# Between pooling and cross-attention: the last token block's norm and transposes, and the first key weights, take other places

## The chip, the cores and the metric

The kernel runs on one core of one Trainium2 chip. The metric is the device time of one execution in microseconds (us); lower is better. Engines are named as the profile names them: PE (matmul and transposes), DVE (vector), ACT (scalar), POOL (GpSimd) and SP, whose queue issues most of the loads.

## The reference, cut to what matters

Two decoder layers run over 512 tokens of 1024 features. Each layer is: half-step feed-forward and norm, token mixer and norm, cross-attention into 256 memory tokens and norm, half-step feed-forward and norm. The mixer of layer 0 is differential attention; that of layer 1 is the pooling mixer. The change lies in layer 1, from the end of its first feed-forward to the first queries of its cross-attention:

```python
def pool_mixer(x, w_grp, b_grp, scale):          # windows 2, 4, 8, 16
    pooled = stack(moving_mean(x, w) for w in windows) - x
    y = einsum('bsgc,gcd->bsgd', pooled, w_grp) + b_grp
    return y.reshape(B, S, D) * scale

x = layer_norm(a * x + pool_mixer(x, ...), ...)

def memory_cross_attention(x, mem, wq, wkv, wo):  # 4 heads of 256
    q = x @ wq;  k, v = split(mem @ wkv, 2)
    p = softmax(q @ k.T * 256 ** -0.5)
    return (p @ v) @ wo
```

## The kernel before, in words

Tokens lie in four blocks of 128 rows, `X[0]` to `X[3]` (in the trace and in the instruction order `X` or `X_74` to `X_77`). All products are made in three passes of float32 that is rounded to the PE's format: an operand is split into a high part, which ACT casts (line 125), and a low part, which DVE gets by subtracting the high part from the source (line 126). So each weight tile costs one cast on ACT (`wh<-raw`) and one subtraction on DVE (`wl<-raw,wh`), and lines 210, 211 and 212 are high by high, high by low of the activations, and low of the weights by high.

A norm of one token block (`ln_token`) is a chain over three engines: DVE makes the mean (line 371), ACT the squares and the variance (lines 379 and 380), POOL the power -1/2 (`rstd`, line 381), and DVE two steps over 128x1024 elements (lines 383 and 385), in place in `X[t]`. Each normalised block then goes through PE transposes (`turn`, line 496, eight of 128x128 for one block) and is split again into `xh` and `xl`, which the query projection reads. `self.late` lists the blocks that have been normalised but not yet transposed; `turn_late(wait)` transposes all of them but the last `wait`.

The pooling mixer of layer 1 needs no transposes of its input. It splits `X[t]` into `xh` and `xl` directly, multiplies by band matrices (`pp`), and then POOL adds a bias to `X[t]` in place (`pool_weights`, line 1356). While its units run, keys and values of the memory for the first heads are made as the main stream (`early_kv`, with `xa_k` for keys and `xa_v` for values): K0, V0, K1, V1, then K2. K0 to V1 below are these weights and products. The mixer's units are woven between. Norms of the mixer are made block by block at the end of `pool_mixer`: for each block two sums, then the transposes of the block before, then the norm of this one. So block 3 is left in `late` when cross-attention begins.

There (`xa_main`) head 0's queries are projected in two column halves of the tokens, blocks 0 and 1 first, blocks 2 and 3 afterwards, each for two output tiles `c`. Between these two halves block 3 is transposed.

The order of instructions on each engine is fixed when the program is built. A scheduler lists them by priority and by its own estimates of when operands are ready. `tc.high_priority()` puts what is issued within it ahead of other ready work; `issue_after` (used by `behind` and `after`) holds an instruction back until another has been listed. In `xa_k` the casts and subtractions of the first head's key weights carry neither; `x_split`, the last split of the mixer's input, holds back those of a head whose `raw` weights were handed in when `then` is not given.

Of the kernel before, what the change touches and what calls it, by code (L numbers as in the profile page):

```python
# [109 lines left out]
class Trunk:  # L110
# [80 lines left out]
    def mm(self, name):  # L191
        return self.mmp.tile([P, S], F32, tag="mm", name=name)
# [1165 lines left out]
    def pool_mixer(self, layer, ln):  # L1358
        nc = self.nc
        bandh, bandf, bandl = self.bandh, self.bandf, self.bandl  # L1360

        self.new_xt()
        xs = [[], []]
        for t in range(NT):
            for half in range(2):
                j = 2 * (t % 2) + half
                x = self.xh[t // 2][:, j], self.xl[t // 2][:, j]
                self.x_split = self.split(x[0], x[1], self.X[t][:, half * S : (half + 1) * S])
                xs[half].append(x)
        pooled = []  # L1370
        mm = nc.tensor.matmul
        yield
        for c in range(KC):
            if c == 1:
                with self.tc.issue_after(split[1].ins):
                    self.pool_weights()
            g = c // 2
            half, o = c // 4, slice((c % 4) * P, (c % 4 + 1) * P)
            pp = self.aux("pp")
            with self.behind():  # L1380
                for t in range(NT):
                    xh, xl = (x[:, o] for x in xs[half][t])
                    n = BAND if t < NT - 1 else P
                    out = pp[:, t * P : t * P + n]
                    m = (bandf if t == 0 else bandh)[:, g, :n]

                    mm(out, xh, m, start=t == 0, stop=False, skip_group_check=True)
                    if t == 0:
                        m0 = bandl[:, g]
                        mm(out[:, :16], xh, m0, start=False, stop=False, skip_group_check=True)  # L1390
                    mm(out, xl, m, start=False, stop=t == NT - 1, skip_group_check=True)
            q = self.pair("pooled")
            split = self.split(q[0], q[1], pp)
            pooled.append(q)
            yield
        wg = self.wide(self.pool_w)
        self.begin_ln(layer, ln, 1.0)
        for t in range(NT):
            o = slice(t * P, (t + 1) * P)
            for half in range(2):  # L1400
                ps = self.aux("ps")
                for j in range(2):
                    g = half * 2 + j
                    for k in range(2):
                        q = pooled[2 * g + k]
                        self.mm3(
                            ps[:, j * 256 : (j + 1) * 256],
                            (q[0][:, o], q[1][:, o]),
                            wg[2 * g + k],
                            k == 0,  # L1410
                            k == 1,
                        )
                self.ln_add(t, half, ALPHA, ps)
                yield
            self.turn_late()
            self.ln_token(t)


    def load_memory(self, tag=None):
# [47 lines left out]
    def xa_k(self, w, h, raw=None, then=None, turn=True):  # L1467
        rk = raw or self.raw_cols(w, h * 256)
        ps = self.mm("pk").rearrange("p (c n) -> p c n", c=2)
        for j in range(2):  # L1470
            with self.after(self.x_split if raw and not then else ()):
                wk = self.cols(rk, j)
            if then and j == 1:
                then()
            for n, k in enumerate(self.mem_order):
                yield self.mm3(
                    ps[:, j], (wk[0][:, k], wk[1][:, k]), self.memT[k], n == 0, n == KC - 1
                )
        kt = self.kv_tiles((P, 2, MEM))
        if turn:  # L1480
            self.turn_late()
        with nullcontext() if turn else self.tc.high_priority():
            self.split(kt[0], kt[1], ps)
        return kt
# [79 lines left out]
    def xa_main(self, layer):  # L1564
        wq, wkv = self.a["xa_wq"][layer], self.a["xa_wkv"][layer]
        early = len(self.kv)
        for h in range(XA_H):
            if h >= len(self.kv):
                self.kv.append((yield from self.xa_kv(wkv, h)))
            kt, v = self.kv[h]  # L1570
            raw = self.raw_cols(wq, h * 256)
            qs = []
            ws = [self.cols(raw, c) for c in range(2)]
            ps = [self.mm("xq") for c in range(2)]
            for p in ((0, 2 * P), (2 * P, S)) if self.late else ((0, S),):
                for c in range(2):
                    yield from self.project(ps[c], ws[c], (p,))
                    self.turn_late(max(len(self.late) - 1, 0) if c == 0 else 0)
            for c in range(2):
                q = self.pair("q")  # L1580
                self.split_scaled(q[0], q[1], ps[c], (D // XA_H) ** -0.5)
                qs.append(q)
            self.heads.append((self.clock, (qs, kt, v)))
            if 0 < early and h + early < XA_H:
                self.kv.append((yield from self.xa_kv(wkv, h + early)))
        yield from self.to_tokens(self.oT, self.a["xa_wo"][layer], 0, 4, True, False, ALPHA)
# [174 lines left out]
```

## Time and profile before

| what | value |
|---|---|
| median of 3 runs | 1916.96 us (1916.87 to 1918.63) |
| the profiled execution | 1915.99 us |
| its span, first to last instruction | 1914.2 us |
| what lies around the span | 1.8 us |
| PE busy | 1898.0 us, 99% of the span |
| DVE busy | 1551.7 us, 81% |
| ACT busy | 1016.6 us, 53% |
| POOL busy | 319.3 us, 17% |
| mean granted PE clock | 0.999 |

The rows of the timeline give the start of an instruction in us from the span's start, its duration in us, the engine, the line, the output and inputs, and, where the engine sat idle before it, how long and for whom. Durations of neighbours overlap a little since engines pipeline; the pace of an engine is the distance from start to start.

### The profile page before, as it was taken

To read this page: it belongs to the slowest core of one execution; us is meant where nothing else is said; L and a number is where in the kernel's file an instruction comes from. 1 tells how busy PE (TensorE), PEld (TensorE's weight loads), DVE (VectorE), ACT (ScalarE), POOL (GpSimd) and SP (SyncE) were. 2 spreads that over 40 slices of the span, in tenths; PEclk is the share of its full clock that TensorE was granted. 3 is DMA by queue.
4 is the path that set the end of the run, shared out by engine and by line. 5 is a ranking of instruction groups with operands and counts; after the bars stand their busy time and mean duration, and the time that the engine had idled before them with its cause. 6 is when DMAs were issued, how large, how long until landed. Compare 5 with 4: busy or idle time off the path is not lost.

```text
span 1914.2 us, 32507 instructions
## 1 busy us (share of the span) xinstructions
PE 1898.0 (99%) x13088; PEld 1732.0 (90%) x13088; DVE 1551.7 (81%) x2250; ACT 1016.6 (53%) x1578; POOL 319.3 (17%) x282
## 2 busy tenths in 40 slices
PE   9999999999999999999999999999999999999998
PEld 8999998888879888999998999999898889999996
DVE  7888889888867558889888988898787568998886
ACT  6555454566745435655553655555455436555552
POOL 3112121111110002221220311212130012211210
PEclk9999999999999999999999999999999999999999
DMA  9978772332225317987785687878344438867861
GB/s 249 215 176 177 177 139 78 91 89 67 89 67 161 116 60 194 193 175 164 143 191 171 117 180 166 181 164 186 101 132 133 137 84 174 178 156 168 189 130 54
DMA packets 246743, 277.96 MB, mean 145 GB/s; under 512 B 8256, under 2 KB 212544, under 8 KB 246592
## 3 DMA queue, kind: packets, MB, share of 16 engines
q0 software_dynamic: 92928, 92.29, 31.5%
q1 hardware_dynamic: 153664, 183.59, 29.9%
q8 instruction: 103, 1.69, 0.4%
q14 instruction: 48, 0.39, 0.1%
HBM read 273.75 MB, written 2.10 MB: 144 GB/s over the span
## 4 chain that ended last, share of the span: by engine, by line
PE 82%; DVE 11%; ACT 3%; DMA 2%; issue 1%; POOL 1%; SPq 0%; DVEq 0%; ACTq 0%; POOLq 0%
PE x L210 7%; PE x L211 7%; PE x L212 7%; PE z L210 4%; PE z L211 4%; PE z L212 4%; PE ps L210 4%; PE ps L212 4%; PE ps L211 4%; PE px L212 2%; PE px L210 2%; PE px L211 2%; PE y L212 2%; PE y L210 2%; PE y L211 2%; PE pz L212 1%
## 5 line engine op out<-in xcount | busy, mean ns | idle before, releaser
L715 POOL DMA_DIRECT2D ra<-in_ffn_w_in_dram x132 | 170.8, 1316 | 981.8 <-DVE wl L722 966.2
L720 ACT CAST wh<-ra 128x1024 fp32r<-128x1024 f32 x176 | 185.1, 1054 | 206.9 <-PE x L211 65.7
L722 DVE TENSOR_TENSOR wl<-ra,wh 128x1024 fp32r<-128x1024 f32 x176 | 214.2, 1222 | 66.5 <-ACT wh L720 66.1
L210 PE MATMUL x<-xe,wh 128*128 128x256 f32 x704 | 194.8, 277 | 0.0
L211 PE MATMUL x<-xe,wh 128*128 128x256 f32 x704 | 194.6, 276 | 0.0
L212 PE MATMUL x<-xe,wl 128*128 128x256 f32 x704 | 194.5, 276 | 0.0
L720 ACT CAST wh<-rc 128x1024 fp32r<-128x1024 f32 x132 | 138.9, 1053 | 101.6 <-PE x L211 41.4
L125 ACT CAST wh<-b 128x1024 fp32r<-128x1024 f32 x112 | 117.8, 1051 | 130.5 <-PE x L211 67.2
L722 DVE TENSOR_TENSOR wl<-rc,wh 128x1024 fp32r<-128x1024 f32 x132 | 160.0, 1220 | 24.9 <-ACT wh L720 24.9
L126 DVE TENSOR_TENSOR wl<-b,wh 128x1024 fp32r<-128x1024 f32 x112 | 136.8, 1221 | 40.2 <-ACT wh L125 40.2
L210 PE MATMUL x<-xh,wh 128*128 128x256 f32 x536 | 148.5, 277 | 0.0
L211 PE MATMUL x<-xl,wh 128*128 128x256 f32 x536 | 148.2, 276 | 0.0
L212 PE MATMUL x<-xh,wl 128*128 128x256 f32 x536 | 148.2, 276 | 0.0
L211 PEld LDWEIGHTS x<-xe,wh 128*128 128x128 f32 x704 | 132.3, 188 | 1.4
L210 PEld LDWEIGHTS x<-xe,wh 128*128 128x128 f32 x704 | 132.1, 188 | 1.3
L212 PEld LDWEIGHTS x<-xe,wl 128*128 128x128 f32 x704 | 132.2, 188 | 0.0
L126 DVE TENSOR_TENSOR wl<-raw,wh 128x1024 fp32r<-128x1024 f32 x64 | 82.2, 1288 | 42.0 <-ACT wh L125 41.2
L211 PEld LDWEIGHTS x<-xl,wh 128*128 128x128 f32 x536 | 100.7, 188 | 0.7
L210 PEld LDWEIGHTS x<-xh,wh 128*128 128x128 f32 x536 | 100.6, 188 | 0.7
L212 PEld LDWEIGHTS x<-xh,wl 128*128 128x128 f32 x536 | 100.6, 188 | 0.0
L125 ACT CAST wh<-raw 128x1024 fp32r<-128x1024 f32 x64 | 66.4, 1048 | 60.6 <-PE xq L211 20.2
L210 PE MATMUL z<-xe,wh 128*128 128x256 f32 x352 | 97.4, 277 | 0.0
(451 smaller groups left out, 6289.7 us busy)
## 6 DMA issues: line engine op xcount, KB each, us to landing
ra<-in_ffn_w_in_dram POOLq DMA_DIRECT2D x132, 512.0 KB, 6.9
rc<-in_ffn_w_in_dram SPq DMA_DIRECT2D x88, 512.0 KB, 5.9
b<-in_ffn_w_out_dram SPq DMA_DIRECT2D x76, 512.0 KB, 4.8
ra<-in_ffn_w_in_dram SPq DMA_DIRECT2D x44, 512.0 KB, 5.0
rc<-in_ffn_w_in_dram POOLq DMA_DIRECT2D x44, 512.0 KB, 7.5
raw<-in_xa_wkv_dram SPq DMA_DIRECT2D x16, 1024.0 KB, 5.4
raw<-in_da_w_qkv_dram SPq DMA_DIRECT2D x16, 512.0 KB, 5.2
raw<-in_xa_wq_dram SPq DMA_DIRECT2D x8, 1024.0 KB, 5.2
```

The lines of the kernel that those rows point to most:

```text
L125: self.nc.scalar.copy(hi, src),
L126: self.nc.vector.tensor_sub(lo, src, hi.bitcast(F32)),
L210: self.first_mm = mm(out, w[0], x[0], start=start, stop=False, skip_group_check=again)
L211: mm(out, w[0], x[1], start=False, stop=False, skip_group_check=again)
L212: self.last_mm = mm(out, w[1], x[0], start=False, stop=stop, skip_group_check=again)
L715: nc.gpsimd.dma_start(t, source(*block), accum_op=ALU.add)
L720: hi = nc.scalar.copy(v[0], raw)
L722: lo = nc.vector.tensor_sub(v[1], raw, v[0].bitcast(F32))
```

## The change

Three edits. In `pool_mixer` the norm of the last token block (`t > 2`) is issued with high priority. In `xa_k` the casts and subtractions of the first early head's key weights (K0, the call with `then`) are issued with high priority. In `xa_main` the remaining late blocks are transposed after the fourth of the eight contraction steps of the second output tile (`c` = 1), and no longer after the eighth.

```diff
@@ pool_mixer
             self.turn_late()
-            self.ln_token(t)
+            with self.tc.high_priority() if t > 2 else nullcontext():
+                self.ln_token(t)
@@ xa_k
         for j in range(2):
-            with self.after(self.x_split if raw and not then else ()):
+            with self.tc.high_priority() if then else self.after(self.x_split if raw else ()):
                 wk = self.cols(rk, j)
@@ xa_main
             for p in ((0, 2 * P), (2 * P, S)) if self.late else ((0, S),):
                 for c in range(2):
-                    yield from self.project(ps[c], ws[c], (p,))
-                    self.turn_late(max(len(self.late) - 1, 0) if c == 0 else 0)
+                    for k, ns in enumerate(self.project(ps[c], ws[c], (p,))):
+                        yield ns
+                        if c and k == 3:
+                            self.turn_late()
+                    if c == 0:
+                        self.turn_late(max(len(self.late) - 1, 0))
```

On DVE, at the end of layer 1's first feed-forward: `wl<-raw,wh` are the lows of K0's two weight tiles (the first two) and V0's two (the last two), `xl<-X_76,xh` the lows of block 2, and `X_77,sums` with `mean` the last sum and the mean of block 3.

```order
-L126 TENSOR_TENSOR wl<-raw,wh 128x1024
-L126 TENSOR_TENSOR xl<-X_76,xh 128x512 x2
-L126 TENSOR_TENSOR wl<-raw,wh 128x1024
+L126 TENSOR_TENSOR wl<-raw,wh 128x1024 x2
+L126 TENSOR_TENSOR xl<-X_76,xh 128x512
 L362 SCALAR_TENSOR_TENSOR X_77,sums<-X_77,ps 128x512
-L126 TENSOR_TENSOR wl<-raw,wh 128x1024
-L371 TENSOR_SCALAR mean<-sums 128x1
-L126 TENSOR_TENSOR wl<-raw,wh 128x1024
+L126 TENSOR_TENSOR xl<-X_76,xh 128x512
+L371 TENSOR_SCALAR mean<-sums 128x1
+L126 TENSOR_TENSOR wl<-raw,wh 128x1024 x2
```

K0's second tile moved ahead of both halves of block 2's lows, the sum came between these halves, and the mean went ahead of both of V0's tiles. ACT casts K0's second tile right behind the first, ahead of block 2's highs.

On DVE, at the start of cross-attention: `xl<-pt` are the lows of transposed blocks 2 and then 3, `X_77` with `mean,gb` and `rstd,gb` the two steps of block 3's norm, `kv<-pk` the lows of K2, and `wl<-raw` first V2's two weight tiles and then one of head 1's query weights.

```order
-L126 TENSOR_TENSOR xl<-pt,xh 128x4x128
+L383 SCALAR_TENSOR_TENSOR X_77<-X_77,mean,gb 128x1024
 L126 TENSOR_TENSOR kv<-pk,kv 128x512
-L126 TENSOR_TENSOR xl<-pt,xh 128x4x128
-L383 SCALAR_TENSOR_TENSOR X_77<-X_77,mean,gb 128x1024
-L126 TENSOR_TENSOR wl<-raw,wh 128x1024
 L385 SCALAR_TENSOR_TENSOR X_77<-X_77,rstd,gb 128x1024
-L126 TENSOR_TENSOR wl<-raw,wh 128x1024
-L126 TENSOR_TENSOR xl<-pt,xh 128x4x128 x2
-L126 TENSOR_TENSOR wl<-raw,wh 128x1024
+L126 TENSOR_TENSOR xl<-pt,xh 128x4x128 x4
+L126 TENSOR_TENSOR wl<-raw,wh 128x1024 x3
```

Ahead of block 3's second step stood two halves of block 2's lows, K2's lows and one weight tile; now only K2's lows stand between its two steps, and the lows of blocks 2 and 3 and V2's tiles follow.

On PE, the same place: `pt` are the transposes of block 3 (`X3_77`), `xq_16221` and `xq_16222` the query tiles `c` = 0 and `c` = 1. Before, they stand behind the last product of the first half of the tokens:

```order
L211 MATMUL xq_16222<-xl_15888,wh_16217 128x256
L212 MATMUL xq_16222<-xh_15886,wl_16218 128x256
L496 MATMUL pt_16247<-ident_78,X3_77 128x128 x4
L496 MATMUL pt_16254<-ident_78,X3_77 128x128 x4
L210 MATMUL xq_16221<-xh_15885,wh_16213 128x256
L210 MATMUL xq_16222<-xh_15885,wh_16217 128x256
L211 MATMUL xq_16221<-xl_15887,wh_16213 128x256
```

Now they stand behind the tenth of the 24 products of `xq_16222` in the first half:

```order
L212 MATMUL xq_16222<-xh_15885,wl_16218 128x256
L210 MATMUL xq_16222<-xh_15885,wh_16217 128x256
L496 MATMUL pt_16247<-ident_78,X3_77 128x128 x4
L496 MATMUL pt_16254<-ident_78,X3_77 128x128 x4
L211 MATMUL xq_16222<-xl_15887,wh_16217 128x256
L212 MATMUL xq_16222<-xh_15885,wl_16218 128x256
```

Fourteen products of `xq_16222` that PE did ahead of the transposes now follow them.

## The prediction

> **What bounds the kernel now.** I read the page first, then PE's timeline at the two places that the change touches, then DVE's, POOL's and ACT's rows beside them. The page says that PE is the bound:
>
> ```profile
> PE 1898.0 (99%) x13088; PEld 1732.0 (90%) x13088; DVE 1551.7 (81%) x2250; ACT 1016.6 (53%) x1578; POOL 319.3 (17%) x282
> ```
>
> So a change of order can only win back moments in which PE stands still, and these are small. At the first place, K0 and K1 on PE:
>
> ```profile
> 1393.96 0.28 PE L211 MATMUL pk<-mem0l,wh 128*128 128x256 f32 x1
> 1394.69 0.39 PE L212 MATMUL pk<-mem0h,wl 128*128 128x256 f32 x1 [0.45 <-DVE wl L126]
> ...
> 1397.39 0.28 PE L210 MATMUL pk<-mem0h,wh 128*128 128x256 f32 x1
> 1397.51 0.28 PE L211 MATMUL pk<-mem0l,wh 128*128 128x256 f32 x1
> 1398.13 0.39 PE L212 MATMUL pk<-mem0h,wl 128*128 128x256 f32 x1 [0.34 <-DVE wl L126]
> ...
> 1408.66 0.28 PE L211 MATMUL pk<-mem0l,wh 128*128 128x256 f32 x1
> 1409.11 0.39 PE L212 MATMUL pk<-mem0h,wl 128*128 128x256 f32 x1 [0.17 <-DVE wl L126]
> ```
>
> The pace is 0.12 us from start to start (1397.39 to 1397.51). PE reaches the low part of a weight tile before DVE has made it three times: for K0's first tile (0.73 instead of 0.12, so 0.61 us lost), for its second (0.62: 0.50 lost) and for K1's first (0.45: 0.33 lost). Together 1.44 us.
>
> At the second place PE ends the first half of head 0's queries and wants block 3's transposes:
>
> ```profile
> 1444.56 0.28 PE L212 MATMUL pk<-mem6h,wl 128*128 128x256 f32 x1
> ...
> 1446.02 0.28 PE L212 MATMUL pk<-mem6h,wl 128*128 128x256 f32 x1
> ...
> 1449.88 0.28 PE L210 MATMUL xq<-xh,wh 128*128 128x256 f32 x1
> ...
> 1451.47 0.28 PE L212 MATMUL xq<-xh,wl 128*128 128x256 f32 x1
> 1452.49 1.09 PE L496 MATMUL pt<-ident,X 128*128 128x128 f32 x8 [0.74 <-DVE X L385]
> ...
> 1454.77 0.28 PE L212 MATMUL xq<-xh,wl 128*128 128x256 f32 x1
> ```
>
> From 1444.56 to 1446.02 PE did eight transposes (block 2's) and two products: 1.46 us with next to no waiting. From 1451.47 to 1454.77 it did eight transposes and three products: 3.30 us. The third product costs 0.11 ((1451.47 - 1449.88) / 14 products), so this stretch would take 1.57 us without waits, and 1.73 us are lost: first to DVE's last step on block 3, then to its highs and lows after the transposes.
>
> **Second place: early norm, transposes amid the first half.** DVE and ACT before:
>
> ```profile
> 1445.90 1.22 DVE L126 TENSOR_TENSOR wl<-raw,wh 128x1024 fp32r<-128x1024 f32 x1
> 1447.04 0.68 DVE L126 TENSOR_TENSOR xl<-pt,xh 128x512 fp32r<-128x512 f32 x1
> ...
> 1448.83 1.27 DVE L383 SCALAR_TENSOR_TENSOR X<-X,mean,gb 128x1024 f32<-128x1024 f32 x1
> 1450.03 1.22 DVE L126 TENSOR_TENSOR wl<-raw,wh 128x1024 fp32r<-128x1024 f32 x1
> 1451.16 1.28 DVE L385 SCALAR_TENSOR_TENSOR X<-X,rstd,gb 128x1024 f32<-128x1024 f32 x1
> ```
>
> ```profile
> 1446.00 0.19 ACT L379 ACTIVATION_READ_ACCUMULATOR sq<-X,mean 128x1 f32 x1
> ...
> 1447.52 0.22 ACT L380 ACTIVATE var<-var 128x1 f32<-128x1 f32 x1
> 1447.62 2.00 ACT L125 CAST wh<-raw 128x1024 fp32r<-128x1024 f32 x2
> 1453.18 0.59 ACT L125 CAST xh<-pt 128x512 fp32r<-128x512 f32 x1 [3.56 <-PE pt L496]
> ```
>
> By the new order the first step on block 3 takes the place of the split at 1447.04; the squares that it has to wait for ended at 1446.19. It paces at 1.20 (1448.83 to 1450.03), K2's lows at 0.60 ((1448.83 - 1447.04) / 3), so the second step starts at 1448.84 and ends 1.28 later, at 1450.12, and no longer at 1452.44. POOL's power stands between: the variance comes one cast earlier, about 1447.1, and the power can be ready when the second step's turn comes (price below).
>
> PE gets to its new place after the product at 1449.88, that is at 1449.99. Against 1450.12 it waits 0.13 at most. The transposes' own work is unchanged. Of the 1.73 us I take 1.7 as won.
>
> What is late next there? The 14 products that now follow the transposes (1.59 us) cover the highs and lows. The highs begin 0.69 after the transposes (1452.49 to 1453.18 before), so at 1450.8; block 2's lows run from 1450.04 to 1451.2, block 3's from about 1451.4 to 1452.7. PE starts the second half at about 1452.8 and first reads only the first half of the features. Some 0.6 us of cover; if it went, PE would wait for just the excess. V2's lows, before at 1450.03 and after, move to about 1452.8 to 1455.0, far ahead of their product:
>
> ```profile
> 1460.40 0.36 PE L210 MATMUL pv<-wh,mem0h 128*128 128x256 f32 x1
> ```
>
> V2's buffer is thus freed some 1.5 us later, and on SP's queue the next load, K3, goes out that much later than here, while ACT casts it 11 us on:
>
> ```profile
> 1453.60 0.37 SPq L238 DMA_DIRECT2D raw<-in_xa_wkv_dram  x1
> ```
>
> ```profile
> 1464.81 1.05 ACT L125 CAST wh<-raw 128x1024 fp32r<-128x1024 f32 x1 [3.31 <-issue]
> ```
>
> With 1.7 us off that cast and 1.5 us on the load, 8 of these 11 us are left for a transfer of 5 to 7: nothing.
>
> **First place: K0 with priority.** DVE and POOL before:
>
> ```profile
> 1393.41 1.22 DVE L126 TENSOR_TENSOR wl<-raw,wh 128x1024 fp32r<-128x1024 f32 x1
> ...
> 1395.75 2.33 DVE L126 TENSOR_TENSOR wl<-raw,wh 128x1024 fp32r<-128x1024 f32 x1
> ...
> 1398.61 1.70 DVE L126 TENSOR_TENSOR wl<-raw,wh 128x1024 fp32r<-128x1024 f32 x1
> ...
> 1401.81 1.28 DVE L383 SCALAR_TENSOR_TENSOR X<-X,mean,hr 128x1024 f32<-128x1024 f32 x1 [0.24 <-ACT sp L379]
> 1403.54 1.29 DVE L385 SCALAR_TENSOR_TENSOR X<-X,rstd,sr 128x1024 f32<-128x1024 f32 x1 [0.44 <-POOL rstd L381]
> ...
> 1406.98 4.30 DVE L126 TENSOR_TENSOR wl<-raw,wh 128x1024 fp32r<-128x1024 f32 x2 [0.17 <-ACT wh L125]
> ```
>
> ```profile
> 1395.38 3.85 POOL L1356 TENSOR_TENSOR X<-X,p 128x512 f32<-128x512 f32 x2 [3.81 <-DVE xl L126]
> 1402.09 1.41 POOL L381 TENSOR_TENSOR rstd<-var,mhalf 128x1 f32<-128x1 f32 x1 [2.86 <-ACT var L380]
> ...
> 1447.88 0.55 POOL L381 TENSOR_TENSOR rstd<-var,mhalf 128x1 f32<-128x1 f32 x1 [4.55 <-ACT var L380]
> ```
>
> K0's first tile is already DVE's next work at 1393.41, behind block 3's first sum, and stays there: its 0.61 us remain. The second follows at once, about 1394.6, and is ready at 1395.8, 1.8 us before PE asks. So the stall of 0.50 goes.
>
> But this is not yet won. DVE's chain here runs on to block 3's first norm, to K1's casts behind it on ACT, and to the low part for which PE waits at 1409.11. Whatever PE gains at 1398 it loses there unless this chain ends earlier too. Its work is the same, so only its delays count. Before: a subtraction that takes 1.22 takes 2.33 and 1.70 while POOL adds the bias to block 2 (1.11 and 0.48 lost), then 0.24 and 0.44 of waiting for ACT and POOL: 2.27 us. After: POOL's first half-add can start only behind the first half of block 2's lows, so it falls on the second half of these lows, and the second half-add on one of V0's two tiles. Each collision cost about 0.9 to 1.1 (4.30 for two that need 2.44: 0.93 each; or 1.11): 1.9 to 2.2 us. The two waits go, since the mean now precedes V0's tiles. So the chain gains 0.1 to 0.4. Against it: the power took 1.41 beside DVE's step and 0.55 alone; if it now lies beside V0's second tile as well, 0.3 to 0.5 us come back. I take +0.1, with bounds of -0.3 and, were all collisions gone, +1.1 (the stalls of 0.50 and 0.33, and 0.3 of the chain).
>
> The Trainium skill ("SBUF — State Buffer", section "Who interferes with whom") says that a DVE instruction with two SBUF inputs and a GpSimd instruction that reads SBUF exclude one another for a whole instruction. The trace agrees: 2.33 against 1.22. By that rule this place is worth about nothing; if the two shared the time evenly and the sums (which read PSUM) hid part of it, the chain would gain 0.8 and the total be 2.5.
>
> K0's buffer is freed about 2.4 us earlier, so SP sends K1's load and those behind it earlier; K1's cast waits for block 3 on ACT and gains nothing by it. ACT's cast of K0's second tile moves into time in which ACT sat idle ahead of block 2's highs. Later in this stage K1's or V1's casts change places with a pooled split by one position; PE shows no wait there: nothing.
>
> **Sum.** 1.7 + 0.1 = 1.8 us. The profiled execution took 1915.99, so 1914.2; the median of the runs lies 0.97 above it, 1916.96, and 1.8 less is 1915.2. A fifth of a percent, 3.83 us, is about what a measurement of this kernel can tell from no change: this forecast lies within it.
>
> **Rivals.**
>
> *Both places pay.* If POOL's adds fall into gaps, the first place gives 1.1 and the sum is 2.8: 1914.2. For it: DVE's sum on PSUM was not slowed beside POOL. Against: POOL's add is released by the very lows that DVE is working on.
>
> *The second place doesn't pay.* PE then waits amid the half as long as it did behind it: about 1916.9. It would need block 3 to be ready at 1451.7 or later, that is 1.6 us lost on DVE or POOL between 1447.0 and 1448.8. Only the power could do it: its 1.41 began beside a step on DVE; even so it is done about 0.6 after that step, when K2's lows end. I find no more than a few tenths.
>
> *Slower: the load of V2 holds ACT.* Block 3's highs stand behind V2's two casts on ACT. Before, they were wanted at 1453.18, now at 1450.8, so that V2's lateness, harmless so far, can hold PE. Its transfer and the spread of all these transfers:
>
> ```profile
> raw<-in_xa_wkv_dram SPq DMA_DIRECT2D x1, 1024.0 KB, 5.3
> ...
> DMA to landing us min/median/max: 5.1/5.4/11.8
> ```
>
> It lands about 0.5 before 1447.62, and two casts take 2.0. PE waits once the casts end after some 1452.2, a landing at 1450.2; the gain of 1.7 is eaten at 1451.9, a transfer of 10. At 11.8 it lands at 1453.6 and the kernel is 1.7 slower than before: 1918.7. Against it: nothing stands ahead of this load, whereas the one of 11.8 had three before it.
>
> **How the numbers follow.** Forecast 0.58, both places 0.15, second place fails 0.13, slower by V2's load 0.08, anything else 0.06. All stalls named come to 1.44 + 1.73 = 3.2 us, under 3.83, so faster by over 0.2% has only the unnamed and the spread of runs: 0.07. Slower by over 0.2% needs a still later load or the unnamed: 0.07. The rest, 0.86, is within 0.2%. The range goes from 1913.6 (3.2 us and a little spread) to 1918.0 (the second place fails and the runs lie as the slowest of before, 1918.63, nearly did).
>
> **What would show it.** Right: K0's second low part is on DVE directly behind the first; PE's wait near 1398 is gone, and a wait near 1409 (for K1's lows, or for block 3's lows in the first `pp` products) takes most of it back; two subtractions between 1396 and 1402 are still stretched to about twice their time; block 3's second step ends some 2.3 us earlier against PE; the transposes start with a wait of under 0.2, and the second half's first products with none. Wrong: transposes that wait for more than 0.5, the second half waiting for `xl` or `xh`, or PE at 1409 earlier than before by more than 0.5.

## The result, and the profile after

The changed kernel takes 1913.84 us (median of 19 runs, 1912.81 to 1915.63), the kernel before beside it 1917.37 (19 runs, 1915.35 to 1919.56); the ratio is 0.9983, with a 95% interval of 0.9976 to 0.9990. That is 3.5 us less by the medians and 1.9 to 4.6 by the interval; the forecast was 1.8. The profiled execution took 1912.81 us instead of 1915.99, its span 1911.0 instead of 1914.2.

The page of the changed kernel shows a PE as busy as before, with 1.6 us less in it:

```profile
span 1911.0 us, 32507 instructions
...
PE 1896.4 (99%) x13088; PEld 1731.1 (91%) x13088; DVE 1551.6 (81%) x2250; ACT 1017.8 (53%) x1578; POOL 319.9 (17%) x282
```

PE's timeline after, first place. The wait for K0's second low (1398.13 before) is gone, the one for its first and the one for K1's first are as they were, and there is a new one for V0's second tile:

```profile
1393.35 0.28 PE L211 MATMUL pk<-mem0l,wh 128*128 128x256 f32 x1
1394.10 0.38 PE L212 MATMUL pk<-mem0h,wl 128*128 128x256 f32 x1 [0.47 <-DVE wl L126]
...
1396.83 0.28 PE L211 MATMUL pk<-mem0l,wh 128*128 128x256 f32 x1
1396.94 0.28 PE L212 MATMUL pk<-mem0h,wl 128*128 128x256 f32 x1
...
1400.80 0.28 PE L210 MATMUL pv<-wh,mem4h 128*128 128x256 f32 x1
1401.32 0.39 PE L211 MATMUL pv<-wl,mem4h 128*128 128x256 f32 x1 [0.25 <-DVE wl L126]
...
1407.69 0.28 PE L211 MATMUL pk<-mem0l,wh 128*128 128x256 f32 x1
1408.14 0.39 PE L212 MATMUL pk<-mem0h,wl 128*128 128x256 f32 x1 [0.17 <-DVE wl L126]
```

From 1393.35 to 1408.14 are 14.80 us by the unrounded times; the same stretch of the program took 15.15 before (1393.96 to 1409.11). So 0.35 us were won here, of the 0.50 that the vanished stall had cost.

The second place on PE after. The transposes begin 0.11 behind the product ahead of them, without a wait, and nothing waits behind them either. One small wait is new, ahead of them: the first product of the second query tile (1448.01):

```profile
1443.60 0.28 PE L212 MATMUL pk<-mem6h,wl 128*128 128x256 f32 x1
...
1448.01 0.39 PE L210 MATMUL xq<-xh,wh 128*128 128x256 f32 x1
...
1449.16 0.28 PE L210 MATMUL xq<-xh,wh 128*128 128x256 f32 x1
1449.27 1.03 PE L496 MATMUL pt<-ident,X 128*128 128x128 f32 x8
1450.06 0.36 PE L211 MATMUL xq<-xl,wh 128*128 128x256 f32 x1
...
1452.15 0.28 PE L210 MATMUL xq<-xh,wh 128*128 128x256 f32 x1
```

The product of 1452.15 is as many matmuls from the start of the program as that of 1454.77 before. From 1443.60 it is 8.54 us by the unrounded times, before (from 1444.56) 10.21: 1.67 won. The new wait costs 0.23 within this stretch: the product of 1448.01 starts 0.23 behind the one ahead and 0.22 ahead of the next, at a pace of 0.11. It ends with DVE's lows of K2 (1447.27 + 0.69 = 1447.96), which now stand behind the first step of block 3's norm.

That makes 2.0 us. Between the two places, and from the second to the last product, the two profiles differ by less than 0.1 us. The third part stands where the change touches nothing: at the very end. The last product, before and after:

```profile
1905.91 0.28 PE L212 MATMUL ps<-ha,xe 128*128 128x256 f32 x1
```

```profile
1903.34 0.28 PE L212 MATMUL ps<-ha,xe 128*128 128x256 f32 x1
```

The span ends 8.3 us behind it before and 7.7 after, though the products and the additions there are the same. The DMA view of the last microseconds, first of before from 1908 to its end, then of after from 1905 to its end (GB/s in 40 slices; then a queue's packets and MB; then the issues and the median time from issue to landing):

```profile
GB/s 0 0 0 0 0 0 0 0 0 0 0 0 0 0 0 0 92 396 410 357 344 199 396 383 396 344 66 13 26 13 0 0 0 0 0 0 0 0 0 0
...
q14 instruction: 1, 0.01, 0.3%
...
out_dram<-X SPq DMA_DIRECT2D x2, 256.0 KB, 2.4
```

```profile
GB/s 0 0 0 0 0 0 0 0 0 0 0 0 0 0 0 0 0 0 0 0 300 423 382 314 410 396 396 355 396 123 0 0 0 0 0 0 0 0 0 0
...
out_dram<-X SPq DMA_DIRECT2D x2, 256.0 KB, 2.1
```

Before, one packet of instructions (queue 14, 8 KB) falls amid the write of the output, 5.6 us behind the start of the last product. After, that queue is silent here: its packet came 1.3 us ahead of the last product. So 0.35 + 1.67 + 0.6 = 2.6 us can be named in the traces. Another 0.6 of the profiled pair lies ahead of 1393.96, where both programs are alike. The profiled kernels below, all with that program, got to this product anywhere from 1391.58 to 1394.78 us, so this is put down to chance.

### The profile page after: what moved, and what is told of

Its sections match the earlier page's. It is cut to its first block, busy times and chain, and to the rows that moved or that the text cites. A ratio compares the mean times of both kernels' runs of the same rounds, so it can differ in the third digit from the quotient of the medians.

```text
span 1911.0 us, 32507 instructions
## 1 busy us (share of the span) xinstructions
PE 1896.4 (99%) x13088; PEld 1731.1 (91%) x13088; DVE 1551.6 (81%) x2250; ACT 1017.8 (53%) x1578; POOL 319.9 (17%) x282
## 4 chain that ended last, share of the span: by engine, by line
PE 83%; DVE 11%; ACT 3%; DMA 2%; issue 1%; POOL 1%; SPq 0%; DVEq 0%; ACTq 0%; POOLq 0%
PE x L210 7%; PE x L211 7%; PE x L212 7%; PE z L210 4%; PE z L211 4%; PE z L212 4%; PE ps L210 4%; PE ps L212 4%; PE ps L211 4%; PE px L210 2%; PE px L212 2%; PE px L211 2%; PE y L212 2%; PE xq L210 2%; PE xq L211 2%; PE xq L212 2%
```

## The experiments

Each stretch below is read from PE's timeline between products of the same number in the program, so what chance did ahead of 1394 doesn't enter. "First place" is 1393.96 to 1409.11 of before, "between" from there to 1444.56, "second place" from there to 1454.77, "end" from the start of the last product to the end of the span (all from unrounded times, so that a last digit can differ from the rows above). The last column compares the runs; the word behind a comma names the kernel that the edit was made to. From the end of the second place to the last product every kernel takes 451.0 to 451.4 us, in no order that follows the edits.

| kernel | first place | between | second place | end | ratio to before |
|---|---|---|---|---|---|
| before | 15.15 | 35.45 | 10.21 | 8.30 | |
| changed | 14.80 | 35.46 | 8.54 | 7.70 | 0.9983 [0.9976, 0.9990] |
| e1 norm alone | 15.14 | 35.45 | 8.49 | 7.72 | 0.9988 [0.9979, 0.9997] |
| e2 K0 alone | 14.80 | 35.45 | 10.22 | 8.31 | 0.9997 [0.9988, 1.0005] |
| e3 transposes alone | 15.14 | 35.46 | 10.22 | 8.30 | 1.0000 [0.9992, 1.0009] |
| e4 changed again | 14.81 | 35.45 | 8.54 | 7.70 | 0.9990 [0.9981, 0.9998] |
| e5 one wait, before | 15.16 | 35.49 | 10.18 | 8.32 | 0.9999 [0.9990, 1.0008] |
| e6 additions late, changed | 13.83 | 35.33 | 8.55 | 7.71 | 0.9979 [0.9970, 0.9988] |
| e7 first low, changed | 14.80 | 35.45 | 8.49 | 7.70 | 0.9982 [0.9974, 0.9991] |
| e8 both, changed | 13.21 | 35.79 | 8.54 | 7.70 | 0.9983 [0.9974, 0.9991] |
| e9 one instruction, before | 15.16 | 35.45 | 10.21 | 7.70 | 0.9994 [0.9985, 1.0004] |
| e10 additions late, before | 13.82 | 36.38 | 10.18 | 8.31 | 0.9996 [0.9986, 1.0006] |
| e11 changed, beside e12 | 14.80 | 35.45 | 8.49 | 7.71 | 0.9990 [0.9981, 0.9999] |
| e12 additions late, beside e11 | 14.18 | 35.32 | 8.49 | 7.72 | 0.9979 [0.9970, 0.9988] |

**The three edits, one by one (e1 to e3), and the whole (e4).** The first:

```diff
-            self.ln_token(t)
+            with self.tc.high_priority() if t > 2 else nullcontext():
+                self.ln_token(t)
```

> Only the norm of block 3 has priority; transposes and K0 are written as before. The order of instructions that this gives is the same on every engine as that of this edit with the edit on the transposes together. Theory A (the gain is the norm's, at the second place; the edit on the transposes moves nothing): PE gains 1.6 us between 1446 and 1461, as in the changed kernel, nothing at the first place; time 1.6 us under before. Theory B (the transposes' place matters): less than half of that, 0.8 us or under. Theory C (part of the measured 3.5 us comes from nowhere near the two places): start and tail differ from before by some tenths again, in either direction.

Measured: 1913.46 us beside 1915.76. The second place gives 1.72 and the end 0.58, the first nothing. So the end belongs to this edit.

The second:

```diff
-            with self.after(self.x_split if raw and not then else ()):
+            with self.tc.high_priority() if then else self.after(self.x_split if raw else ()):
```

> Only K0's casts and subtractions have priority. Theory A (DVE's collisions with POOL give back most at K1): PE's wait for K0's second tile goes (0.5 us), PE is 0.3 us ahead of before after K1's first tile, nothing more later; time 0.3 us under before, within noise. Theory B (the first place carries what the two profiles don't show): 1.5 us or more under before.

Measured: 1915.11 us, not to be told from before by the runs; by the stretches 0.34 at the first place and nothing anywhere else. PE's waits from 1380 to 1470 (us in all, how many, the longest) show the trade, two waits for K0 and K1 and a new one for V0, with block 3 waited for as ever:

```profile
PE pt L496 <- DVE X L385: 0.8, 1, 0.8
PE pk L212 <- DVE wl L126: 0.6, 2, 0.5
PE pv L211 <- DVE wl L126: 0.3, 1, 0.3
```

The third is the edit in `xa_main` alone:

```diff
-                    yield from self.project(ps[c], ws[c], (p,))
-                    self.turn_late(max(len(self.late) - 1, 0) if c == 0 else 0)
+                    for k, ns in enumerate(self.project(ps[c], ws[c], (p,))):
+                        yield ns
+                        if c and k == 3:
+                            self.turn_late()
...
```

> Only the transposes of block 3 are written after the fourth step of the second query tile. The scheduler gives the same order of instructions on every engine as before, so this is before once more: theory A: no change, within 0.5 us, and every wait of before; the profile's start (first 12 us) and tail differ from before's by up to 0.7 us all the same, which tells how much of the difference of two profiles is chance. Theory B (the edit on the transposes does something that the order doesn't show): a change of 0.5 us or more at 1450.

Measured: 1915.63 us, ratio 1.0000, all four stretches as before. The order of instructions of this kernel is that of before on every engine, and in the trace of e1, which lacks the third edit, PE's order is that of the changed kernel from first to last. So it is the norm's priority that moved the transposes on PE: the scheduler lists them when it believes block 3 to be ready, wherever the code asks for them.

The changed kernel once more, beside these:

> The changed kernel once more. Theory A (two places, 1.9 us; the rest of 3.5 is chance): the comparison on one chip gives 1.5 to 2.5 us under before, PE is again 0.3 and 1.6 us ahead at the two places, and start and tail differ from the first profile by some tenths. Theory B (the change moves start or tail too): 3 us or more under before again, with the same 0.7 us in the first 12 us and 0.6 in the tail.

Measured: 1913.10 us, ratio 0.9990, and the stretches of the first time. By the stretches the parts add up: 0.34 (e2) + 1.72 and 0.58 (e1) = 2.6; the whole gives 0.34 + 1.67 + 0.60 = 2.6.

**What shortens the end (e5, e9).** The trace of before has 607 instructions on SP, that of the changed kernel and of e1 has 608: the load of K3, sent at 1454.15, waits for one semaphore more, by an instruction of its own at 1447.28. e5 gave the kernel before one more wait on SP, on the load of head 0's query weights for a pooled cast (`cast_2`):

```diff
...
+            if layer == 1 and h == 0:
+                info = mybir.DependencyInfo(mybir.DependencyClass.Sync, mybir.DependencyReason.DATA)
+                self.tc.add_manual_dep(self.last_load.ins, self.cast_2.ins.name, info, reason="one_more_wait")
```

> Before, with one more wait on SP's queue: the load of head 0's query weights also waits for a cast on ACT that ended 1.5 us earlier, so nothing starts later and every engine's order is that of before. The changed kernel too has one instruction more on SP than before. Theory A (the 0.6 us by which the changed kernel's end after PE's last product is shorter comes from where a block of SP's instructions is fetched: in before this fetch falls amid the write of the output, with one instruction more it comes ahead of it): the end after the last product takes 7.1 us and not 7.7, the fetch of 8 KB on queue 14 lies ahead of the last product, all else as before, time 0.6 us under before. Theory B (the end is shorter because the norm's order changed): 7.7 us as before, no change in time.

Measured: 1915.53 us, the end 8.32. (The expectation's 7.7 and 7.1 count to an event of SP some 0.6 ahead of the end of the span; they are the 8.3 and 7.7 of the table.) This does not decide, since the trace still has 607 instructions on SP: that load had two waits, and a third one went into an instruction that was there already. In the changed kernel it was a load with three waits that got a fourth. e9 did just that, on another load (the twentieth from line 238, sent at 1401.60 in before), for the last cast of weights ahead of it, with the order on all engines as before:

```diff
...
+        if self.loads == 20:
+            info = mybir.DependencyInfo(mybir.DependencyClass.Sync, mybir.DependencyReason.DATA)
+            self.tc.add_manual_dep(self.last_load.ins, self.last_cast.ins.name, info, reason="one_more_wait")
...
```

> The kernel before, with one more wait on the load that already waits for three things (the second head's first load of keys and values after the early ones, at 1401.6 in the trace of before); a fourth wait costs SyncE an instruction of its own, so that SyncE runs 608 instead of 607. The order on every engine is that of before. Theory A (the 0.58 us at the end hang on how many instructions SyncE has run: with one more, its next 8 KB of instructions are fetched before the last products instead of amid the write of the output): from the start of the last product to the end of the last instruction 7.7 us as in the changed kernel instead of 8.3, the fetch some 1.3 us ahead of that product instead of 5.6 us after it, and nothing else, so about 0.6 us under before. Theory B (the end is shorter because block 3's part of the program got shorter or because PE reached the end earlier): 8.3 us and no change.

Measured: 608 instructions on SP, the end 7.70, the other stretches as before to 0.02 us. The runs give 1914.36 beside 1916.01, ratio 0.9994 [0.9985, 1.0004]; 0.6 us is 0.9997, so they neither confirm nor exclude it, and the trace decides. Its last product, the DMA view of the stretch just ahead of it (1901.5 to 1903.4) and of the end:

```profile
1903.42 0.28 PE L212 MATMUL ps<-ha,xe 128*128 128x256 f32 x1
```

```profile
q14 instruction: 1, 0.01, 1.3%
```

```profile
out_dram<-X SPq DMA_DIRECT2D x2, 256.0 KB, 2.1
```

The packet lies ahead of the last product and the write lands in 2.1 us, as in the changed kernel. The other traces fit: the five with 607 instructions on SP have the packet 5.6 us behind the last product and an end of 8.30 to 8.32, the nine with 608 have it 1.2 to 1.4 ahead and an end of 7.70 to 7.72. So 0.6 us of the change's gain came from one instruction more on SP, whatever this instruction does. How the packet slows the end isn't settled. The last output packet ends 0.50 us earlier without it, which is most of the 0.6. SP sends the second half of the write 0.08 later with it (4.59 behind the last product in before, 4.51 after), and this half takes 2.56 us to land instead of 2.04, so most of the loss lies in the transfer; what in it is held up was not tried.

**What holds the first place (e6, e7, e8, e10).** e6 holds POOL's additions to blocks 2 and 3 back until the first pooled split:

```diff
...
-                nc.gpsimd.tensor_tensor(x, x, bs, ALU.add)
+                add = nc.gpsimd.tensor_tensor(x, x, bs, ALU.add)
+                if t > 1:
...
+                    self.tc.add_manual_dep(add.ins, behind.ins.name, info, reason="bias_late")
...
```

> The changed kernel, with POOL's bias adds on blocks 2 and 3 held back until K1's low parts and the first pooled split are done on DVE (nothing is left out). Theory A (these adds exclude DVE's subtractions with two operands in SBUF and so gave back most of the first place's gain): the three stretched subtractions, 1.47, 3.46 for two and 4.30 for two, take 0.7, 2.4 and 2.4; PE's waits for V0's second tile (0.4) and K1's first (0.33) go; PE is 0.8 us further ahead at 1410 than in the changed kernel; time 0.8 us under it unless the adds then stretch V1's tiles. Theory B (the stretching has another cause): unchanged durations, no gain.

Measured: 1911.67 us beside 1915.63. DVE's and POOL's timelines (first place) and PE's waits from 1380 to 1470:

```profile
1394.83 0.68 DVE L126 TENSOR_TENSOR xl<-X,xh 128x512 fp32r<-128x512 f32 x1
...
1395.56 2.35 DVE L126 TENSOR_TENSOR wl<-raw,wh 128x1024 fp32r<-128x1024 f32 x2
...
1402.66 2.36 DVE L126 TENSOR_TENSOR wl<-raw,wh 128x1024 fp32r<-128x1024 f32 x2 [0.18 <-ACT wh L125]
...
1405.54 5.80 DVE L1352 TENSOR_TENSOR pw<-pw,p 128x512 f32<-128x512 f32 x4
```

```profile
1405.70 6.81 POOL L1356 TENSOR_TENSOR X<-X,p 128x512 f32<-128x512 f32 x4 [7.39 <-DVE pooled L126]
```

```profile
PE pk L212 <- DVE wl L126: 0.5, 1, 0.5
```

All three subtractions are back to 0.68, 2.35 and 2.36, and of PE's waits only K0's first is left; the stretch is 13.83. The collision has moved to the four multiplications of line 1352, which nothing waits for soon (5.80 us here; in the changed kernel, the row below, 2.48). Theory A holds, and the gain over the changed kernel, 0.97 at this place, is larger than the 0.8 that it gave.

```profile
1410.84 2.48 DVE L1352 TENSOR_TENSOR pw<-pw,p 128x512 f32<-128x512 f32 x4
```

e7 takes K0's first wait instead:

```diff
...
+            if then and j == 0:
+                self.queue_behind(self.sum_of_3, self.last_pair[1])
```

> The changed kernel, with the low part of K0's first tile put ahead of block 3's first sum on DVE. Theory A (K0's first tile was left waiting behind this sum, and DVE's chain to K1 decides what remains): PE's wait for K0's first low part (0.62) falls to 0.1 or less; but V0's second tile and K1's first come no earlier, so PE's waits there grow by as much and it is at most 0.1 ahead of the changed kernel at 1410. Theory B (each stall counts by itself): 0.6 us ahead at 1410 and in time.

Measured: 1912.56 us; the stretch is 14.80, as in the changed kernel. K0's wait is gone and V0's, 0.2 in the changed kernel, is 0.6 (lines are one further down in this kernel):

```profile
PE pv L212 <- DVE wl L126: 0.6, 1, 0.6
PE pk L213 <- DVE wl L126: 0.2, 1, 0.2
```

So a stall that goes here comes back at the next low part: it is the length of DVE's chain that sets the end of the stretch.

e8 has both edits:

> The changed kernel with both: K0's first low part ahead of block 3's first sum, and POOL's adds on blocks 2 and 3 held back. Theory A: all four waits of PE between 1393 and 1410 go, PE is 1.4 us ahead of the changed kernel at 1410 and stays so; time 1.4 us under it, some 4 us under before. Theory B (POOL's adds hurt elsewhere, amid V1's tiles or the pooled splits): PE's gain at 1410 is lost again by 1425.

Measured: 1912.16 us. The first place is 13.21, the best of all, but the stretch behind it takes 35.79 instead of 35.33, since PE then waits for a later low. First place and between come to 49.00 (e6: 49.16). So of the 1.6 us by which PE is ahead of the changed kernel at the end of the first place (14.80 less 13.21), 1.25 stay: theory A in the main. Of the 0.62 that e7's edit adds to e6's there, three quarters are lost again, as theory B has it.

e10 is e6's edit on the kernel before:

> The kernel before, with GpSimd's two bias additions to blocks 2 and 3 held back until the first pooled split, and neither of the change's edits. Theory A (the additions beside the subtractions of keys' and values' lows are what costs at 1395 to 1411, whichever order these stand in): VectorE's 2.33, 1.70 and 4.30 us become 1.2, 1.2 and 2.4, TensorE's waits at 1398.3 (0.50) and 1409.1 (0.45) go, and TensorE is 0.8 to 1.0 us ahead at 1410; of the 1.44 us that the changed kernel with this edit gained there, the priority is then worth about 0.5. Theory B (the order of the lows sets it): the wait at 1398.3 stays at 0.5, and TensorE is 0.45 us ahead at most. Time: 0.5 to 1.0 us under before.

Measured: 1914.81 us beside 1916.01, ratio 0.9996 [0.9986, 1.0006]. At the first place it is as good as e6 (13.82; more than either theory said). Then the stretch behind it takes 36.38: first place and between are 50.20 against 50.60 before. The line-1352 multiplications and a wait on PE (1410 to 1430) show why:

```profile
1409.10 5.78 DVE L1352 TENSOR_TENSOR pw<-pw,p 128x512 f32<-128x512 f32 x4
```

```profile
PE ps L211 <- DVE wl L126: 0.5, 1, 0.5
```

In the order of before the same delay of DVE reaches a low part that PE wants. So the two edits need each other: over first place and between, priority alone gives 0.34, late additions alone 0.39, both together 1.43 (e6; 1.09 in e12).

**The best version beside the changed kernel (e11, e12).** Both on one chip, in one series:

> The changed kernel once more, beside the next one, on the same chip: by the places in the traces (0.33 us at the first, 1.66 at the second, 0.58 at the end) 2.6 us under before, if these are all that it gains; 3.5 if the first comparison was right and something is still missing from the list. In its trace the three places give the same again, whatever the stretches ahead of 1394 do.

> The changed kernel with GpSimd's two additions held back, once more, beside the changed kernel: 1.44 us instead of 0.33 at the first place, the second and the end as in the changed kernel, so 3.7 us under before and 1.1 under the changed kernel. A rival (its first comparison owed something to chance ahead of 1394): the same trace at the places, and a difference of the times that lies anywhere from 0 to 2 us.

Measured: 1914.12 us and 1911.87 beside 1915.43 for before. The changed kernel with POOL's additions late is 2.3 us under it by the medians; by the stretches it is 0.61 and 0.12 in these two traces, 0.98 and 0.12 between e4 and e6, so 0.7 to 1.1. The difference of the medians is more than the stretches name, and the intervals of the ratios (up to 3.6 and 5.7 us under before) leave room for both.

## Why the prediction was right, and by how much not

The forecast, 1.8 us under before, is right in direction, and the time is inside the range, 0.2 us above its lower end. The two places give 2.0 us, by the mechanism that was forecast; the 0.6 at the end is luck, and 0.9 more stays unexplained. By its steps:

**Second place, 1.7: right.** 1.67 to 1.73 in the eight traces with the first edit. The path was the one described, but for one wait: PE stands 0.23 us at the second query tile until DVE has made K2's lows, and so comes to the transposes later than supposed and finds block 3 ready. The prediction gave K2's lows a place behind the first step and did not ask who wants them; instead it allowed 0.13 at the transposes. DVE's rows after:

```profile
1446.08 1.28 DVE L383 SCALAR_TENSOR_TENSOR X<-X,mean,gb 128x1024 f32<-128x1024 f32 x1
1447.27 0.69 DVE L126 TENSOR_TENSOR kv<-pk,kv 128x512 fp32r<-128x512 f32 x1
1447.87 1.28 DVE L385 SCALAR_TENSOR_TENSOR X<-X,rstd,gb 128x1024 f32<-128x1024 f32 x1
```

The second step ends at 1449.15, by PE's own place 2.3 us earlier than before (1452.44 less the 0.96 that PE is ahead), as forecast. POOL's power did start beside the first step and took 1.33, ended at 1447.76, and held nothing back:

```profile
1446.43 1.33 POOL L381 TENSOR_TENSOR rstd<-var,mhalf 128x1 f32<-128x1 f32 x1 [4.06 <-ACT var L380]
```

The change's third edit, which asks for the transposes at that place, moved nothing: the first did (e3, e1).

**First place, 0.1: too small, 0.34 to 0.35 in the traces with the second edit and POOL's additions in their old place.** The terms of the prediction give -0.4 to +0.1 (0.1 to 0.4 won, 0.3 to 0.5 lost), so +0.1 was their upper end and not their middle. The frame was right: the collisions with POOL stay, and DVE's chain to K1 sets the gain (e7). The terms of that chain, with DVE's and POOL's rows after and, last, DVE's row of V0's second tile before:

```profile
1392.82 2.36 DVE L126 TENSOR_TENSOR wl<-raw,wh 128x1024 fp32r<-128x1024 f32 x2
...
1396.30 1.47 DVE L126 TENSOR_TENSOR xl<-X,xh 128x512 fp32r<-128x512 f32 x1
...
1397.81 3.46 DVE L126 TENSOR_TENSOR wl<-raw,wh 128x1024 fp32r<-128x1024 f32 x2
1401.19 1.27 DVE L383 SCALAR_TENSOR_TENSOR X<-X,mean,hr 128x1024 f32<-128x1024 f32 x1
1402.58 1.28 DVE L385 SCALAR_TENSOR_TENSOR X<-X,rstd,sr 128x1024 f32<-128x1024 f32 x1
...
1406.02 4.30 DVE L126 TENSOR_TENSOR wl<-raw,wh 128x1024 fp32r<-128x1024 f32 x2 [0.18 <-ACT wh L125]
```

```profile
1397.91 2.28 POOL L1356 TENSOR_TENSOR X<-X,p 128x512 f32<-128x512 f32 x1 [0.69 <-DVE mean L371]
1400.14 1.53 POOL L381 TENSOR_TENSOR rstd<-var,mhalf 128x1 f32<-128x1 f32 x1
```

```profile
1400.36 1.21 DVE L126 TENSOR_TENSOR wl<-raw,wh 128x1024 fp32r<-128x1024 f32 x1
```

The collisions cost 1.47 - 0.69 = 0.78 and 3.46 - 2.35 = 1.11, together 1.9, the low end of the forecast 1.9 to 2.2. The power came back as foreseen, stretched to 1.53 beside V0's second tile and the first step, but cost the second step only 0.19 (1402.58 instead of 1401.19 + 1.20), not 0.3 to 0.5. And the two waits that go were worth 0.85 on DVE's pace, not 0.68: V0's second tile to the first step 1.45 instead of 1.14 (1400.36 to 1401.81), the first step to the second 1.73 instead of 1.20. In all 1.6 + 0.85 = 2.45 us of delay before and 2.1 after; from K0's first low to K1's first it is 13.57 before (1393.41 to 1406.98) and 13.20 after. The mis-sized terms are the power, 0.1 to 0.3 too dear, and the waits, 0.17 too cheap.

**Where it comes back: the wrong tile.** K1's wait near 1409 was to take back most of the stall that goes at 1398. It stays at 0.45, as before. What took most back was V0's second tile, at 1401.32 (0.52 behind the product ahead, so 0.4 lost), behind the second stretched subtraction. PE's stalls alone don't add up to the 0.35, since PE's own pace differs between these two profiles (0.118 before, 0.114 after; see the last section); e1, with the order of before and a pace of 0.113, lost 0.60 at K0's second tile. PE's waits after, from 1380 to 1470:

```profile
PE pk L212 <- DVE wl L126: 0.6, 2, 0.5
PE pv L211 <- DVE wl L126: 0.2, 1, 0.2
```

The prediction saw that POOL's second addition would fall on one of V0's tiles, but had no term for PE's wait there, where before there was none.

**The end, 0.6: not in the prediction.** The sum had no term for the instructions that a wait itself costs: in the new order K3's load waits for a fourth semaphore, and what that does is seen only in the number of SP's instructions and in the packets at the end (e9). That these 0.6 us are a gain and not a loss is luck.

**The rivals.** Both places pay in full (2.8): not so, as long as POOL's additions lie there (e6 is that case). The second place fails, or V2's load holds ACT: in no trace with the first edit does PE wait for block 3 or for its highs there. The same two subtractions take 2.36 without POOL and 4.30 beside it, and the four multiplications 2.48 and 5.80 (e6, e10). In e6's trace the two engines take turns: each multiplication but the first ends 0.55 us behind the end of an addition, and each addition 1.15 to 1.17 behind the end of a multiplication. By the Trainium skill ("SBUF — State Buffer", section "Who interferes with whom") a DVE instruction with two SBUF inputs and a POOL instruction that reads SBUF contend for ports that one of them locks; the trace agrees. That "about nothing" was too low for this place lies in the sizes named above, of the waits and the power.

What is left of the 3.5 us in the medians, 0.9 over the 2.6 that the traces name, stays unexplained; the comparisons of e4 and e11 (1.9 us each by the ratio) fall on the other side, and 2.6 lies in all three intervals.

## What to carry to other kernels

Where PE catches up with a chain on another engine, a stall that is taken out moves to the next tile unless the chain itself gets shorter: cost the chain's delays from start to start, not the stall. Two small moves can need each other (0.34 and 0.39 alone, 1.1 to 1.4 together), so try them as a pair before dropping either. And compare the ends of both traces, from the last product on, even if the change is far from there.

## What was not expected of the hardware

- One instruction more on SP, some 500 us ahead of the end, shortened the end by 0.6 us; with it an 8 KB packet of instructions moved out of the write of the output (e9: end 7.70 instead of 8.30). In this kernel, then, an edit that changes the number of SP's instructions can carry 0.6 us that has nothing to do with what it is for.
- The same products run at two paces. In e6 and e12, which are the same program with the same one wait, those of K0 and V0 go at 0.113 and at 0.118 us from start to start; the first place takes 13.83 and 14.18. Where PE waits for DVE this doesn't show: before ran them at 0.118 and e1, with the same order here, at 0.113, and the stretch is 15.15 and 15.14, since a faster PE waits longer. What sets the pace is open.
